# Moving the waits for the last stores from SyncE to GpSimd in an RMSNorm + ReLU kernel

## Chip, cores, metric

The kernel runs on one core of one Trainium2 chip. The metric is the device time of one execution in microseconds (us), lower is better. Names: SyncE is SP in the profile, ScalarE ACT, VectorE DVE, GpSimd POOL, TensorE PE; a q behind the name means the engine's sequencer.

## The reference

```python
# x: (16, 1024, 512) float32, gamma: (512,) float32, eps: 1e-5
def reference(x, gamma, eps):
    rms = np.sqrt(np.mean(x ** 2, axis=-1, keepdims=True) + eps)
    x_norm = x / rms * gamma
    return np.maximum(x_norm, 0).astype(np.float32)
```

It reads 33.6 MB and writes 33.6 MB, with little arithmetic.

## The kernel before

The rows are cut into 8 chunks of 4 MB. Six slots in the on-chip memory hold a chunk each. SyncE issues all loads of x and all stores. ScalarE sums the squares, VectorE scales in place and applies the ReLU. GpSimd has no arithmetic: it only turns landed loads into counts for ScalarE. Each slot has one semaphore, raised by 16 for its load and by 16 for its store, so slots that are used once end at 32, slots used twice at 64.

```python
    def store(i):
        nc.sync.dma_start(out=ov[i], in_=slot_ap(i)).then_inc(sem_slot[i % nslots], 16)

    ctx.enter_context(tc.manual_schedule(engines={mybir.EngineType.SP}))
    with tc.tile_critical():
        for m, (i, a, r) in enumerate(loads):
            if i < nslots:
                load(m)
        nxt = nslots
        for i in range(nchunks):
            nc.sync.wait_ge(done, per * (i + 1))
            store(i)
            ...                      # the loads of chunks 6 and 7
        for m, (i, a, r) in enumerate(loads):
            loaded(nc.gpsimd, m)
            nc.gpsimd.sem_inc(ready, r // G)
        ...                          # ScalarE and VectorE
            nc.vector.tensor_scalar_max(out=blk, in0=blk, scalar1=0.0).then_inc(done, 1)

    with nc.sync.register("landed") as landed:
        nc.sync.reg_mov(landed, 32)
        for s in range(nchunks - nslots, nslots):
            nc.sync.wait_ge(sem_slot[s], landed)
        nc.sync.reg_mov(landed, 64)
        for s in range(nchunks - nslots):
            nc.sync.wait_ge(sem_slot[s], landed)
```

The last lines hold the program until every store has landed. Behind them the framework adds its closing: every engine drains and reports to a barrier that GpSimd collects, GpSimd clears the semaphores of the kernel, and a second barrier lets all go.

## Time and profile before

| what | value |
|---|---|
| time, median of 3 runs | 162.84 us (162.62 to 162.89) |
| span of the profiled run | 160.9 us |
| share of the store and load queue in the span | 97.6% |
| last packet of the last store ends | 159.397 us |
| sixteenth increment of its semaphore ("the landing") | 159.875 us |
| end of the span | 160.904 us |

The time is some 1.8 us longer than the span (162.69 against 160.9 in the profiled one); that part lies outside the program. The lines of the profile are in the prediction below. The three times from "last packet" on are read from single records of the trace, which has them in ns; the views round starts to 0.1 us.

### The profile page before, as it was taken

What the parts mean: (1) busy time and instruction counts of PE and PEld (TensorE: products, weight loads), DVE (VectorE), ACT (ScalarE), POOL (GpSimd) and SP (SyncE); (2) the same over time, 40 slices, a digit from 0 to 9 for tenths busy, and PEclk for the clock granted to TensorE, in tenths of its full rate; (3) what the DMA queues carried; (4) which work ended last, traced back from release to release, by engine and by line L of the source; (5) the groups of instructions that cost most, each with busy time, mean ns of one, the idle gap of its engine ahead of it and who ended that gap; (6) DMA issues with size and microseconds to landing.
All of it is one profiled execution on the core that took longest, in us unless ns stands there. A gap on an engine that the chain in (4) does not pass through costs nothing. (4 is left out here: it accounts for less than half of the span.)

```text
span 160.9 us, 1006 instructions
## 1 busy us (share of the span) xinstructions
DVE 126.0 (78%) x164; ACT 86.3 (54%) x273; POOL 0.2 (0%) x4
## 2 busy tenths in 40 slices
DVE  1103989898989899999999999999999999994000
ACT  3088929889988988988900198503994000000000
POOL 0000000000000000000000000000000000000000
DMA  5999999999999998999999999999999999999993
GB/s 155 434 432 415 521 391 391 513 399 391 489 424 391 481 432 367 415 391 489 424 391 489 424 391 448 464 391 440 456 407 432 456 415 424 464 415 424 464 407 138
DMA packets 2456, 67.12 MB, mean 417 GB/s; under 512 B 276, under 2 KB 276, under 8 KB 280
## 3 DMA queue, kind: packets, MB, share of 16 engines
q1 hardware_dynamic: 2448, 67.11, 97.6%
q10 hardware_dynamic: 8, 0.01, 0.0%
HBM read 33.56 MB, written 33.55 MB: 417 GB/s over the span
## 5 line engine op out<-in xcount | busy, mean ns | idle before, releaser
L124 ACT ACTIVATE junk<-slots 128x512 f32 x128 | 74.5, 582 | 30.6 <-ACTq L120 30.3
L148 DVE SCALAR_TENSOR_TENSOR slots<-slots,rstd,gamma_sb 128x512 f32 x128 | 86.2, 747 | 4.8 <-DVEq L145 4.8
L155 DVE TENSOR_SCALAR slots<-slots x16 | 36.7, 2294 | 2.4 <-DVEq L154 0.2
L124 ACT ACTIVATION_READ_ACCUMULATOR junk<-slots x128 | 23.9, 187 | 0.0
L142 DVE RECIPROCAL rstd<-rms x16 | 3.1, 196 | 6.3 <-DVEq L138 6.3
L131 ACT ACTIVATE rms<-ss,eps_sb x16 | 4.8, 301 | 3.0 <-ACTq L130 3.0
L135 DVE LOAD_MASK_SELECT gamma_sb<-gseed x1 | 0.0, 14 | 5.8 <-DMA gseed<-in_gamma_dram 5.8
L116 ACT ACT_TABLE_LOAD x1 | 1.3, 1283 | 2.8 <-issue 2.8
L109 DVE MEMSET gseed<- 128x512 f32 x1 | 0.5, 485 | 1.1 <-SPq L90 1.1
L135 DVE STREAM_SHUFFLE gamma_sb<-gseed 128x512 f32<-128x512 f32 x1 | 0.7, 715 | 0.0
L180 POOL MEMSET const-bfloat16-1.0<- 128x1 bf16 x1 | 0.1, 103 | 0.0
L180 POOL MEMSET const-uint8-127<- 128x1 uint8 x1 | 0.1, 102 | 0.0
L180 POOL MEMSET const-float32-0.0<- 128x1 f32 x1 | 0.1, 100 | 0.2 <-issue 0.2
L180 POOL MEMSET const-float32-1.0<- 128x1 f32 x1 | 0.1, 99 | 0.0
L110 DVE MEMSET eps_sb<- 128x1 f32 x1 | 0.1, 59 | 0.0
## 6 DMA issues: line engine op xcount, KB each, us to landing
out_dram<-slots SPq DMA_DIRECT2D x8, 4096.0 KB, 31.3
slots<-in_x_dram SPq DMA_DIRECT2D x7, 4096.0 KB, 30.3
slots<-in_x_dram SPq DMA_DIRECT2D x2, 2048.0 KB, 9.6
gseed<-in_gamma_dram ACTq DMA_DIRECT2D x1, 8.0 KB
```

The source lines that it names most:

```text
L109: nc.vector.memset(gseed, 0.0).then_inc(sem_z, 1)
L110: nc.vector.memset(eps_sb, eps).then_inc(sem_z, 1)
L116: nc.scalar.preload_act_table(ACTF.Sqrt)
L124: a = nc.scalar.activation(out=junk[:, j, :], in_=slots[:, bass.ds(base + j * d, d)], func=ACTF.Square, accum_out=ss[:, bass.ds(col + j, 1)])
L131: nc.scalar.activation(out=rms[:, bass.ds(col, G)], in_=ss[:, bass.ds(col, G)], func=ACTF.Sqrt, bias=eps_sb, scale=inv_d).then_inc(sq, 1)
L135: nc.vector.stream_shuffle(gamma_sb, gseed, [0] * 32)
L142: nc.vector.reciprocal(out=rstd[:, bass.ds(col, G)], in_=rms[:, bass.ds(col, G)]).then_inc(sv, 1)
L148: r = nc.vector.scalar_tensor_tensor(out=row, in0=row, scalar=rstd[:, bass.ds(col + j, 1)], in1=gamma_sb, op0=ALU.mult, op1=ALU.mult)
L155: nc.vector.tensor_scalar_max(out=blk, in0=blk, scalar1=0.0).then_inc(done, 1)
L180: nc = _bacc.Bacc("TRN2", target_bir_lowering=False, num_devices=1)
```

## The change

If GpSimd itself waits for the last stores, the message from SyncE to GpSimd ("the stores are done") is no longer needed.

```diff
--- before.py
+++ after.py
@@ -86,7 +86,7 @@
     def store(i):
         nc.sync.dma_start(out=ov[i], in_=slot_ap(i)).then_inc(sem_slot[i % nslots], 16)
 
-    ctx.enter_context(tc.manual_schedule(engines={mybir.EngineType.SP}))
+    ctx.enter_context(tc.manual_schedule(engines={mybir.EngineType.Pool}))
     with tc.tile_critical():
         for m, (i, a, r) in enumerate(loads):
             if i < nslots:
@@ -154,13 +154,13 @@
             nc.vector.sem_inc(sv, -1)
             nc.vector.tensor_scalar_max(out=blk, in0=blk, scalar1=0.0).then_inc(done, 1)
 
-    with nc.sync.register("landed") as landed:
-        nc.sync.reg_mov(landed, 32)
+    with nc.gpsimd.register("landed") as landed:
+        nc.gpsimd.reg_mov(landed, 32)
         for s in range(nchunks - nslots, nslots):
-            nc.sync.wait_ge(sem_slot[s], landed)
-        nc.sync.reg_mov(landed, 64)
+            nc.gpsimd.wait_ge(sem_slot[s], landed)
+        nc.gpsimd.reg_mov(landed, 64)
         for s in range(nchunks - nslots):
-            nc.sync.wait_ge(sem_slot[s], landed)
+            nc.gpsimd.wait_ge(sem_slot[s], landed)
 
 
 # ---- launch: one core; inputs and outputs as the reference has them ----
```

The `manual_schedule` line names the engine whose instructions the framework must leave in program order; it has to follow the waits.

## The prediction

> **What bounds the kernel now.** I read four views, from coarse to fine: the page of the profile, the waits of SyncE's queue, three stretches around the end, and the instructions of the lines that the diff or the closing of the program touches.
>
> The page first:
>
> ```profile
> span 160.9 us, 1006 instructions
> DVE 126.0 (78%) x164; ACT 86.3 (54%) x273; POOL 0.2 (0%) x4
> DMA  5999999999999998999999999999999999999993
> ...
> DMA packets 2456, 67.12 MB, mean 417 GB/s; under 512 B 276, under 2 KB 276, under 8 KB 280
> q1 hardware_dynamic: 2448, 67.11, 97.6%
> ...
> out_dram<-slots SPq DMA_DIRECT2D x8, 4096.0 KB, 31.3
> ```
>
> SyncE's one queue keeps the 16 DMA engines occupied for 97.6% of the span, with a digit of 9 (once 8) in every slice but the first and the last. VectorE is at 78% and idles at the end. So the kernel is a stream of 67.1 MB (33.6 in, 33.6 out), and no engine's work sets the time. The change touches only what comes after that stream. The page's own "chain that ended last" is of no help: it starts from the last counted work, a VectorE instruction, and gives 1% of the span, because waits and DMA issues are not counted as busy.
>
> How long is the stretch after the stream? Three windows (us; VectorE, ScalarE and GpSimd busy; clock, DMA share, GB/s):
>
> ```profile
> 144.00:157.00 13.00, 2.29 (x1) 0.00 (x0) 0.00 (x0) 1.00 1.00 434
> 157.00:159.40 2.40, 0.00 (x0) 0.00 (x0) 0.00 (x0) 1.00 0.51 218
> 159.40:160.90 1.50, 0.00 (x0) 0.00 (x0) 0.00 (x0) 1.00 0.00 0
> ```
>
> The last packet of the last store ends at 159.4, and nothing moves in the last 1.50 us. That is an upper bound of what any change of the closing could touch. The trace's semaphore record narrows it: the sixteenth increment of the last store's semaphore arrives at 159.875, that is 0.48 us after the last packet. What the program itself does after the landing is 160.904 - 159.875 = 1.03 us, 0.6% of the time.
>
> Who waits there (waits of SyncE's queue; us in total, times, longest) and what runs there:
>
> ```profile
> SPq L163 <- DMA out_dram<-slots: 12.4, 1, 12.4
> SPq L194 <- PEq L194: 0.6, 2, 0.5
> ...
> L163 SPq EVENT_SEMAPHORE  x1: 17/17/17, 159.9 to 159.9; - x1
> ...
> L194 SPq DRAIN  x2: 7/7/7, 160.1 to 160.2; - x2
> L194 SPq COMPARE_BRANCH  x1: 33/33/33, 159.9 to 159.9; - x1
> ...
> L194 POOLq EVENT_SEMAPHORE  x4: 17/17/17, 160.2 to 160.8; - x4
> L194 POOLq DRAIN  x3: 34/34/88, 147.0 to 160.6; - x3
> ...
> L194 POOLq EVENT_SEMAPHORE_RANGE_CLEAR  x1: 138/138/138, 160.5 to 160.5; - x1
> ```
>
> The reader is to see that the 12.4 us of SyncE's wait is the transfer of the last store, not a cost of waiting; that after it SyncE does a wait, a branch and two drains; and that GpSimd was already at its own closing drain at 147.0, so it stands in the barrier for 13 us. Going through the trace record by record (start times in us), the path from landing to end is: SyncE wait 159.892; branch 159.949 (it carries the other wait, and lasts 33 ns); drain 160.101; second drain 160.161, which signals the barrier; GpSimd takes the signal 160.194 and answers 160.272; GpSimd drain 160.353 (88 ns), range clear of the semaphores 160.470, drain 160.643; second barrier 160.721 and 160.800; TensorE leaves last, 160.853 plus 51 ns. GpSimd is the collector of the barrier already: all others report to it and it alone clears the semaphores.
>
> **What the Trainium skill says.** "Advanced Engine Details and Errata", section "Control Flow Timing", gives a compare-and-branch about 108 ns. Here the branch starts at 159.949 and the next instruction at 160.101, so 152 ns, one wait included; I use 152. "Perfetto Trace Analysis", section "Sequencer-only Instruction (DRAIN, etc)", says that a record shows only the execution, and that the wait before it and the propagation of the semaphore after it are hidden; this is why I count from start to start, not durations (17 ns for a wait, but 57 ns from it to the next instruction). "DMA: Bandwidth & Descriptors", section "Anatomy of one DMA", says the fixed cost of a DMA is mostly the confirmation of the write, heaviest for HBM. The 0.48 us from last packet to last increment agrees in kind, and no engine that waits can shorten it.
>
> **The change part by part.** Removed from SyncE: two register moves (43 and 29 ns), and waits on six semaphores. Four of the six had landed long before: their records lie at 147.24 to 147.44, 12 us ahead of the landing, so they are off the path. Added to GpSimd: the same two moves and waits. GpSimd finishes its part of the section at about 147.0, so its moves and early waits also finish near 147.5 and are off the path. Loads, stores, their order and the arithmetic are as before. What is left on the path:
>
> 1. Waking. SyncE's wait started 17 ns after the last increment (159.875 to 159.892). GpSimd's waits on loads in this trace start 24 ns after theirs (8.320 to 8.344; 91.456 to 91.480; 110.988 to 111.012). Cost: +7 ns.
> 2. Wait to branch, 57 ns, and branch to the next instruction, 152 ns. I assume that the last of the two waits again rides on the branch at the end of the block, now GpSimd's. GpSimd's branch at the program's start lasts 33 ns, as SyncE's does. Change: 0.
> 3. Removed: SyncE's two drains and the hop to GpSimd, from 160.101 to 160.194, 93 ns. Saving: 93 ns.
> 4. Added: GpSimd's own closing drain, which lay at 147.0 and now comes after the wait. From such a drain of 34 ns to the barrier's wait after it takes 78 ns (160.643 to 160.721). The other engines have reported by then. Cost: +78 ns.
> 5. From there on the answer, the clearing and the second barrier, 0.71 us from 160.194, are the same instructions on the same engines. Change: 0.
>
> Sum: 7 - 93 + 78 = -8 ns. The hop that the change takes away is real, but GpSimd's own drain takes nearly all of it back. The change is -0.005% of 162.84 us: nothing that a clock with a spread of 0.27 us (162.62 to 162.89) can see.
>
> **The rivals.**
>
> *The branch goes away.* SyncE alone has a second branch in the closing; GpSimd, ScalarE and VectorE go from the section's drain straight to the closing drain (GpSimd 146.879 to 146.982, 103 ns, with no branch). If GpSimd keeps no branch, about 60 ns from wait to drain would stand in place of 152, and the end comes some 0.1 us earlier: about 162.74. Against it: SyncE's branch seems to be kept because it carries a wait, and the same waits are on GpSimd now. I give this a quarter.
>
> *The wait on SyncE comes back.* The first closing drain of SyncE waits for a semaphore with which the framework collects the end of the work. If the framework now makes it wait for GpSimd's last instruction, there is GpSimd to SyncE to GpSimd instead of one hop. If it runs beside GpSimd's branch (SyncE drains at about 160.00 and 160.06) it is hidden behind the 160.19 of GpSimd. If it comes after the branch, add a signal of 37 ns, SyncE's 60 and the 33 to GpSimd, against GpSimd's 78: about +0.05 us, 162.9. The drain might also take 88 ns, as the one after a barrier does, and not 34: again +0.05 us.
>
> *The stream moves.* What the change could do of any size is to shift the DMAs: were SyncE or GpSimd held up at the start, the first load, issued at 0.94, would come later and all 160 us behind it. The section's entry is a SyncE instruction at 0.714 that releases the others; if the framework gave that to GpSimd, a hop of some 50 to 80 ns would be added once, about 162.9. The order of stores is held by VectorE's signals and can't change. That packets arrange themselves otherwise from run to run is in the spread already.
>
> *A large gain* would need the clearing to overlap with the last store, or the 0.48 us of confirmation to vanish. Neither is in the change: the clear still follows the wait, and must. Even the whole 1.03 us after the landing would be 0.6%, under the 2% line.
>
> **Range and chances.** The working gives -0.01 us, the rivals -0.10 to +0.10; weighted I take -0.04, so 162.8 us. The runs of before spread by 0.27 us, and a median of a few runs may lie 0.15 us off, on either side of the comparison; adding the rivals' 0.1 gives about 0.3 us each way: 162.45 to 163.15. Faster by over 2% would be 3.3 us, three times all that follows the landing: 0.5%. Slower by over 2% needs a broken stream, for example an added wait ahead of SyncE's issues: 1%. Within 2%: 98.5%.
>
> **What would show it.** Right: the span stays within 0.2 us of 160.9; the wait for the last store is GpSimd's, starting about 24 ns after the last increment; SyncE's closing drains lie near 147.3; GpSimd shows a branch, then a drain, and its barrier wait starts 0.31 us after the landing (0.32 before); landing to end is 1.02 us (1.03 before); queue share 97 to 98%. Step 2 is wrong if GpSimd has no branch after the wait, step 4 if its drain takes much over 34 ns, step 5 if the clearing changes its length. The whole is wrong if the last landing itself moves by more than 0.3 us, or if SyncE's first issue is not at 0.94.

## The result, and the profile after

The changed kernel took 162.93 us (median of 6 runs, 162.77 to 163.5); before, beside it, took 162.80 us (6 runs, 162.62 to 163.12). The ratio is 1.001, with a 95% interval of 0.9992 to 1.0029: the same.

The page of the changed kernel (span; DMA share in tenths in 40 slices; the store and load queue; issues of stores):

```profile
span 161.2 us, 1006 instructions
...
DMA  5999999999999999999999999999999999999993
...
q1 hardware_dynamic: 2448, 67.11, 97.6%
...
out_dram<-slots SPq DMA_DIRECT2D x8, 4096.0 KB, 31.5
```

The stream is as it was: same bytes, same share, as many instructions. Only the span is 0.3 us longer. The same stretches around the end, after:

```profile
144.00:157.00 13.00, 2.29 (x1) 0.00 (x0) 0.00 (x0) 1.00 1.00 431
157.00:159.40 2.40, 0.00 (x0) 0.00 (x0) 0.00 (x0) 1.00 0.57 246
159.40:161.20 1.80, 0.00 (x0) 0.00 (x0) 0.00 (x0) 1.00 0.00 0
```

The last 13 us before 157 moved at 431 GB/s where it was 434, and more bytes were left for the stretch after (246 GB/s against 218). The last packet of the last store ended at 159.682 us, 0.285 later than before, and the landing came 0.285 later too. So the 0.3 us arose in the stream, ahead of the code that was changed. That the waits did move is seen in the waits of SyncE's queue (us in total, times, longest):

```profile
SPq L194 <- PEq L194: 13.8, 2, 13.4
```

and the instructions of the wait (L163) and of the closing (L194):

```profile
L163 POOLq EVENT_SEMAPHORE  x1: 17/17/17, 160.2 to 160.2; - x1
...
L194 SPq DRAIN  x3: 7/7/7, 147.2 to 160.7; - x3
L194 POOLq DRAIN  x3: 34/34/88, 160.4 to 160.9; - x3
L194 POOLq COMPARE_BRANCH  x2: 33/33/33, 0.8 to 160.2; - x2
...
L194 SPq COMPARE_BRANCH  x1: 33/33/33, 0.8 to 0.8; - x1
L194 POOLq EVENT_SEMAPHORE_RANGE_CLEAR  x1: 138/138/138, 160.7 to 160.7; - x1
```

The reader is to see the exchange of roles. SyncE's first closing drain starts at 147.2 instead of 160.1, and SyncE then stands 13.4 us in the barrier. The wait is GpSimd's, and so is the second branch. SyncE's 12.4 us of waiting have not gone, they have another name.

Record by record, counted in ns from the landing, in the first profile of each kernel and in a second one from the experiments:

| start of | before | before, again | after | after, again |
|---|---|---|---|---|
| wait for the last store | 17 | 16 | 24 | 24 |
| branch | 74 | 73 | 85 | 85 |
| the waiting engine's closing drain | 226 | 226 | 233 | 233 |
| SyncE's second drain | 286 | 286 | (at 147.3 us) | (at 147.4 us) |
| GpSimd's wait for the barrier | 319 | 318 | 312 | 312 |
| GpSimd's clearing of the semaphores | 595 | 595 | 588 | 588 |
| end of the span | 1029 | 1028 | 1022 | 1022 |

The changed stretch is 6 to 7 ns shorter, and it repeats to 1 ns. The landing itself does not: it lay at 159.875 and 160.241 us with the kernel before, and at 160.160 and 160.105 with the changed one.

### The profile page after: what moved, and what is told of

The parts are those of the page before. It is cut to its first block, busy times and chain, and to the rows that moved or that the text cites. A ratio compares the mean times of both kernels' runs of the same rounds, so it can differ in the third digit from the quotient of the medians.

```text
span 161.2 us, 1006 instructions
## 1 busy us (share of the span) xinstructions
DVE 126.0 (78%) x164; ACT 86.3 (54%) x273; POOL 0.2 (0%) x4
```

## The experiments

My theory was the sum of the prediction: the change exchanges SyncE's two drains and the hop to GpSimd (93 ns) for GpSimd's own drain (78 ns), and what the times differ by is the wandering of the stream. The first rival: waiting on GpSimd slows the stream, and the 0.13 us are real. The second: the hop is what counts, and a wait on the engine that clears is the best place for it. A third question was what in the 1.03 us has any weight. All runs gave correct results.

| run | time, median us | before in the same rounds | ratio (95%) | landing, us | landing to end, us |
|---|---|---|---|---|---|
| before_again | 162.87 | 162.74 | 1.0003 (0.999 to 1.0016) | 160.241 | 1.028 |
| after_again | 162.91 | 162.74 | 1.0002 (0.9989 to 1.0015) | 160.105 | 1.022 |
| gp_inc | 162.70 | 162.74 | 1.0006 (0.9988 to 1.0023) | 159.929 | 0.882 |
| act_inc | 162.70 | 162.74 | 0.9996 (0.9983 to 1.0009) | 159.988 | 0.846 |
| gp_32inc | 165.08 | 162.75 | 1.0137 (1.01 to 1.0175) | 159.781 | 3.311 |
| sp_32inc_off | 162.84 | 162.75 | 1.0 (0.9963 to 1.0037) | 159.978 | 1.022 |
| sp_inc | 162.70 | 162.75 | 0.999 (0.9942 to 1.0037) | 159.887 | 0.888 |
| act_wait | 162.75 | 162.75 | 0.9986 (0.9938 to 1.0033) | 159.989 | 0.988 |

The intervals of the last four are wider because one run of before among their 11 took 164.53 us. Only the interval of gp_32inc is clear of 1; its 1.4% lies under the 2% line.

### before_again: the kernel before against itself

No edit.

> The kernel before once more, unchanged, timed against itself. Both theories: ratio 1.000 with an interval that holds 1; from the last increment of the last store's semaphore to the end of the span 1.03 us (1.029 in the first trace). The theory of a wandering stream expects the landing itself to move by some 0.2 to 0.3 us between profiles of the same kernel, as it moved between before (159.875) and after (160.160). The rival, that GpSimd's waiting slows the stream by about 0.13 us, expects the landing of before to stay within some 0.1 us of 159.875.

Measured: 162.87 against 162.74 us. That is the same 0.13 us by which the changed kernel had seemed slower, here between two copies of one program. The landing lay at 160.241, 0.37 us later than in the first profile. The rival that wants a steady landing for the kernel before is out.

### after_again: the changed kernel, more rounds

No edit.

> The changed kernel once more, with more rounds. Wandering stream: ratio to before within 0.999 to 1.001, the interval holds 1; landing to end 1.02 us again (1.022 in its first trace). Rival (waiting on GpSimd slows the stream): ratio about 1.001 with an interval clear of 1.

Measured: ratio 1.0002, its interval holds 1 (the medians, 162.91 and 162.74 us, are again further apart than the means); landing to end 1.022 us. Over all ten profiles (gp_32inc too, since the landing comes ahead of its additions), the five in which GpSimd waited landed at 159.99 us on average, the five in which another engine waited at 160.00. Neither number speaks for a stream that GpSimd slows. It isn't excluded, though: over all runs of the two sessions in which it was timed, the changed kernel averages 162.91 us (11 runs) and before 162.81 (22, the copies of before_again included), and the standard error of that difference of 0.10 is 0.08 us. An effect of 0.1 us is neither shown nor ruled out.

### gp_inc: take the wait off GpSimd's branch

```diff
         for s in range(nchunks - nslots):
             nc.gpsimd.wait_ge(sem_slot[s], landed)
+        nc.gpsimd.sem_inc(sem_z, 1)
```

(A plain no-operation there was dropped in the build, so I used an increment of a semaphore that nobody reads any more.)

> The changed kernel with one semaphore increment on GpSimd behind the last wait, so that the block's closing branch carries no wait. If the branch of 152 ns stood there only because it carried a wait, GpSimd goes from the wait straight to its drain: landing to end 1.022 - 0.061 - 0.148 + 0.061 = about 0.87 us, that is 0.15 us less. If branches are kept anyway, it stays at 1.02 or more. On the time at most -0.15 us, ratio 0.999, hardly to be told from 1.

Measured: landing to end 0.882 us, 0.140 less than the 1.022 of the changed kernel. GpSimd's closing drain starts 94 ns after the landing, where it was 233. Instructions of GpSimd at the closing and at the wait (now L195 and L164):

```profile
L195 POOLq DRAIN  x3: 34/34/88, 160.0 to 160.6; - x3
L195 POOLq COMPARE_BRANCH  x1: 33/33/33, 0.8 to 0.8; - x1
...
L164 POOLq EVENT_SEMAPHORE  x1: 9686/9686/9686, 150.3 to 150.3; - x1
```

The only branch left is the one at the program's start. The increment took both last waits on itself. Its record is 9.7 us long because it begins when the first of the two semaphores is satisfied (150.3) and ends when the second is. A record with two waits thus shows the second wait in its length; what the prediction took from the skill, that a record hides the wait before it, holds here for the first wait alone. An increment and a drain now stand where a wait, a branch and a drain stood, so the 139 ns are the price of one instruction less, which is a branch. No run puts another instruction in the branch's place; gp_32inc below finds 78 ns for each further increment there, so somewhat over half of the 139 may be what any instruction costs (an estimate). On the time it is nothing that can be seen (ratio 1.0006).

### act_inc: the waits on ScalarE, no branch

The edit is shown against the changed kernel:

```diff
-    ctx.enter_context(tc.manual_schedule(engines={mybir.EngineType.Pool}))
+    ctx.enter_context(tc.manual_schedule(engines={mybir.EngineType.Activation}))
...
-    with nc.gpsimd.register("landed") as landed:
+    with nc.scalar.register("landed") as landed:
...                                # all waits and moves likewise
+        nc.scalar.sem_inc(sem_z, 1)
```

> The waits on ScalarE instead, with one increment behind them so that no branch carries a wait. ScalarE's closing drain lasts 8 ns and it has one where SyncE has two. Wake about 20 ns, wait to drain about 60, drain to GpSimd's answer about 35: GpSimd's barrier wait starts about 0.12 us after the landing, where it was 0.32 in before and 0.31 in after; landing to end about 0.83 us. Cost theory by steps: this is the shortest closing of all. A theory that what counts is to have no hop between engines would expect GpSimd with the same increment (0.87) to be shorter than this.

Measured: landing to end 0.846 us, the shortest of all, although there is a hop from ScalarE to GpSimd again. ScalarE's drain starts at 95 ns, practically where GpSimd's did in gp_inc (94). From the drain to GpSimd's barrier wait it is then 41 ns with ScalarE, hop included, and 78 with GpSimd itself. The rival "no hop is best" is refuted for this kernel. As a version to use it is 0.18 us shorter at the end than before, by the trace; by the clock (ratio 0.9996) it is the same.

### gp_32inc: is this stretch on the path at all?

```diff
             nc.gpsimd.wait_ge(sem_slot[s], landed)
+        for _ in range(32):
+            nc.gpsimd.sem_inc(sem_z, 1)
```

> The changed kernel with 32 semaphore increments on GpSimd behind the last wait (the first rides on the wait, as in the run with one). If this stretch is on the path that sets the end, each of the 31 further ones adds its start-to-start time, 50 to 78 ns by GpSimd's waits in the traces so far, one for one: landing to end 0.882 + 31 x 0.05 to 0.078 = 2.4 to 3.3 us, ratio to before 1.009 to 1.014, clear of 1. If something else (the postamble, another engine) sets the end, much less.

Measured: landing to end 3.311 us, so 2.43 us for 31 increments, 78 ns each. The time rose to 165.08 us, 2.17 us over the changed kernel's 162.91; landing to end had grown by 2.29 in the profiles. So time spent here counts one for one, within the spread of the landing (this profile's lay 0.32 to 0.38 us ahead of those of the changed kernel). Instructions of the added line (L165), here and in the next run:

```profile
L165 POOLq EVENT_SEMAPHORE  x32: 17/17/9686, 150.1 to 162.2; - x32
```

This run is also a lesson on durations: each record but the first lasts 17 ns, but the next one starts 78 ns later.

### sp_32inc_off: the same on the engine that no longer waits

```diff
-    ctx.enter_context(tc.manual_schedule(engines={mybir.EngineType.Pool}))
+    ctx.enter_context(tc.manual_schedule(engines={mybir.EngineType.Pool, mybir.EngineType.SP}))
...
             nc.gpsimd.wait_ge(sem_slot[s], landed)
+        for _ in range(32):
+            nc.sync.sem_inc(sem_z, 1)
```

(Without SyncE in that set the framework moved the increments to the front of the program, where they raced with VectorE's; that version was not run.)

> The changed kernel with the same 32 increments on SyncE, which no longer waits for the stores. They run from about 147.2, some 2 us long, 10 us ahead of the landing, so nothing should change: landing to end 1.022 us, ratio 1.000. If SyncE still took part in the end behind its wait, landing to end would grow.

```profile
L165 SPq EVENT_SEMAPHORE  x32: 17/17/17, 147.2 to 149.1; - x32
```

Measured: landing to end 1.022 us, ratio 1.0. Two microseconds of instructions cost nothing where there are ten to spare, and SyncE's way to the first barrier is no longer on the path. (It still takes part in the second barrier.)

### sp_inc: take the wait off SyncE's branch in the kernel before

```diff
             nc.sync.wait_ge(sem_slot[s], landed)
+        nc.sync.sem_inc(sem_z, 1)
```

> The kernel before with one increment on SyncE behind its last wait, so that SyncE's branch carries no wait either. If the gain seen with GpSimd (0.14 us) belongs to the branch and not to the engine, it comes here too: SyncE's wait to its first drain about 0.08 us in place of 0.226, landing to end about 0.88 us. Without a branch SyncE and GpSimd should again lie within some 10 ns of each other (0.882 for GpSimd). If the gain belongs to GpSimd, it stays at 1.03.

Measured: landing to end 0.888 us, 0.14 less than before. SyncE's first drain starts 86 ns after the landing, and SyncE's own list has no branch after the wait:

```profile
L195 SPq DRAIN  x3: 7/7/7, 160.0 to 160.3; - x3
L195 SPq EVENT_SEMAPHORE  x2: 17/17/17, 160.2 to 160.7; - x2
```

The gain comes with the missing branch, whichever of the two engines waits. With the branch gone on both sides, SyncE and GpSimd are 6 ns apart (0.888 and 0.882), as they were with it (1.028 and 1.022): the change under study is worth the same 6 ns either way.

### act_wait: ScalarE with the branch

The edit of act_inc without its last line.

> The waits on ScalarE, without the increment, so with the branch. ScalarE has one closing drain of 8 ns where SyncE has two and GpSimd one of 34 ns: its drain about 0.23 us after the landing, GpSimd's barrier wait about 0.27 (0.319 with SyncE, 0.312 with GpSimd), landing to end 0.98 us. If the saving of the hop were what counts, GpSimd (1.022) would be the shortest of the three.

Measured: landing to end 0.988 us. The branch is there (ScalarE in the stretch from 159 us on):

```profile
L194 ACTq DRAIN  x2: 8/8/8, 160.2 to 160.5; - x2
...
L194 ACTq COMPARE_BRANCH  x1: 38/38/38, 160.1 to 160.1; - x1
```

ScalarE's drain starts 237 ns after the landing and GpSimd's barrier wait at 278. With SyncE it was 319, with GpSimd 312. The order is set by what an engine must do between the end of its wait and GpSimd's barrier wait: SyncE's two drains and a hop (93 ns), GpSimd's one drain (79), ScalarE's one drain and a hop (41).

## Why the prediction was right

The prediction gave 162.8 us, in a range of 162.45 to 163.15; measured were 162.93, and 162.91 in the repetition. By its own steps:

| step | predicted, ns | measured, ns |
|---|---|---|
| 1. waking, GpSimd for SyncE | +7 | +7 (17 to 24) |
| 2. wait to branch to drain | 0 | 0 (57 + 152 to 61 + 148) |
| 3. SyncE's drains and the hop go | -93 | -93 (226 to 319) |
| 4. GpSimd's drain comes on the path | +78 | +79 (233 to 312) |
| 5. barrier, clearing, second barrier | 0 | 0 (710 and 710) |
| sum | -8 | -7 |

The mechanism and its sizes held, and it is these steps in the trace that test it: that 162.93 us fell into a range 0.7 us wide would also have happened with a change of ten times the size or of none. Of the rivals in it, the lost branch did not happen, for the reason that it gave: the built program lets one of the two last waits ride on the branch, whichever engine waits. (It is the wait for chunk 6's store, which had landed at 150.205 us in the first profile of before, so the branch's 152 ns are not waiting.) Experiments gp_inc and sp_inc took that wait off and the branch went, for 0.14 us. The prediction had guessed 0.1 because of a slip: it set its 60 ns from wait to drain against the 152 from branch to drain, and not against the whole 57 + 152 = 209 from wait to drain, which would have given 0.15. The wait on SyncE did not come back: SyncE's drains are at 147.2. The stream's start is unmoved: the first load was issued at 0.938 us (0.941 before).

Some things were less good. One of the prediction's own signs of being right failed: the span was to stay within 0.2 us of 160.9 and came out 0.28 us longer, all of it ahead of the landing. I had leaned by 0.04 us towards faster for the sake of the rivals, and the runs give no ground for that. I had bounded the movement of a landing by 0.3 us as a sign of error; two profiles of the unchanged kernel differ by 0.37 us, so that test was too sharp. And the early waits were misread a little: the record at 147.24 us is the first register move, and the four waits ride on the records from 147.32 to 147.44; nothing hangs on it.

What stays open: the 7 ns are shown by the traces, in two profiles each, but no clock here can show them; the clock shows only that the difference is below some 0.3%. Why the stream's end wanders by up to 0.46 us between executions (159.781 to 160.241 over ten profiles) was not looked into. The records show only that the landing hangs on the last of its sixteen increments, which came 0.08 to 0.77 us after the fifteenth.

## What to carry to other kernels

Before moving a wait, count from start to start what stands between the end of that wait and the end of the program, and count the work that the new engine must now do in the same place: an engine that was early because it had nothing to wait for has its own closing instructions to bring. A stretch of 1 us in 163 can't pay more than 0.6% whatever is done to it, so a look at the last landing in the trace decides whether such a change is worth a try. And two copies of one kernel on the same chip, run beside the comparison, tell at once what 0.1 us is worth.

## What the Trainium skill lacked or had wrong

- "VectorE: DVE Perf Modes", section "The DRAIN you can't avoid", says of the drains that the runtime adds that they are a constant of about 12 ns on all five engines. It gives no figure for the drains of the framework's closing, which are neither constant nor 12 ns in these traces: 7 ns on SyncE, 8 on ScalarE and TensorE, 10 on VectorE, 34 or 88 on GpSimd. What ate the gain here is the 79 ns from the start of GpSimd's drain of 34 ns to its next instruction; an increment of 17 ns takes the same 78 there (gp_32inc), so the longer record alone doesn't explain it.
- "Advanced Engine Details and Errata", section "Control Flow Timing", gives about 51 ns for a branch that is always taken and 108 for a compare-and-branch. From the start of the closing compare-and-branch, which carries a wait long satisfied, to the next instruction it took 152 ns on SyncE, 148 on GpSimd and 161 on ScalarE. Taking the wait off the branch removed it, and 0.14 us from landing to end.
- No page that I read gives the time from the last packet of a store that SyncE issues to the last increment of its semaphore: 0.43 to 0.48 us in all ten profiles.
- No page that I read has the distance between two semaphore instructions of a sequencer: 78 ns from one increment to the next on GpSimd (31 in a row), about 59 on SyncE, against 17 ns that each record lasts.
